# First pair's gates, k, q and v on four quarters of the tokens; x normed in place on VectorE

## The chip, the cores and the metric

The kernel runs on one core of a Trainium2 chip. What counts is its device time in microseconds (us), from one launch to its end; lower is better. The engines named below are TensorE (PE: matmuls and transposes by the identity; PEld is its weight load), VectorE (DVE), ScalarE (ACT), GpSimd (POOL) and SyncE (SP), whose queue issues the DMA transfers.

## The reference

One decoder layer for 1024 tokens of width 1024, in float32. The part that matters here is its beginning: the tokens are RMS-normed, projected by `w_in`, and the FoX heads attend with a forget bias.

```
h = rms_norm(x, g_attn[l])          # x * rsqrt(mean(x*x) + eps) * g
z = h @ w_in[l]
(fq, fk, fv, f_logit, nq, kc, vc, ksl, vsl, kwn, vwn, n_gate, g_a, g_b) = jnp.split(z, offsets, axis=-1)
o_fox = fox_attention(fox_h(fq), fox_h(fk), fox_h(fv), f_logit, b_forget[l])
...
log_f = jax.nn.log_sigmoid(f_logit + b_f)        # in fox_attention
c = jnp.cumsum(log_f, axis=1).transpose(0, 2, 1)
s = jnp.einsum('bhqd,bkhd->bhqk', qi, k) * SCALE + ci[..., None] - c[:, :, None, :]
```

The second branch (NSA), the merge, the squared-ReLU MLP and the final norm follow; the change does not touch them.

## The kernel before

Every float32 product is made from a high and a low part (`float32r`), in three passes: low weights by high data, high by low, high by high. The normed tokens stand transposed in `hT`: `hTh[0]`, `hTl[0]` hold the high and low part of tokens 0 to 511 (half 0), `hTh[1]`, `hTl[1]` those of half 1; each is 128 partitions by 8 blocks of the width by 512 tokens.

`phase_a` makes `hT`. For each of eight tiles `i` of 128 tokens, x is loaded; `xg = x * g` is made, fifteen of the sixteen half rows on GpSimd; ScalarE squares x with a running sum, and `rstd` and `newton` make the factor `r` of each token by five small VectorE instructions (`v`, `y`, `t`, `t`, `r`) of one column. For tiles 0 to 2 (`NDIAG`), a diagonal matrix `by = identity * r` is made and the transposing matmul multiplies by it; for the others VectorE scales `xg` by `r`, and TensorE transposes by the identity `idn`. `turn_tile` then copies four 128x128 blocks at a time from PSUM (tile `tn_...`, two banks) to `hTh` on ScalarE and subtracts on VectorE for `hTl`.

A `Steps` list holds pieces of TensorE work with a cost each. `gates` (the forget and NSA gate logits, tile `g`), `k_pair` (`fk`), `q_pair` (`fq`) and `v_pair` (`fv`) fill the lists `qa`, `qb`, `s1` for the first pair of heads. `proj` does 24 matmuls for one projection of 512 tokens; with `parts=2` it does them as two sets of 24 with 256 tokens each. Before, half 0 of the gates, k and q is done in such quarters: quarter 0 (tiles 0, 1) in `qa`, quarter 1 (tiles 2, 3) in `qb`; half 1 and all of v stand in `s1`, 512 tokens wide. `phase_a` runs `qa` beside tiles 2 and 3, and `qb` beside tiles 4 to 7; `s1` follows. The raw weights come by DMA (`wload`, two buffers `wr`) and are split into `wh_...` on ScalarE and `wl_...` on VectorE (`wsplit`).

A scheduler orders the instructions of each engine from the order of the code and these lists; at run time each engine works through its own row in that order and waits at its head. After the first pair's projections, `attend` interleaves the attention of the heads (scores `sf`, softmax `pf`, transposes `ptf`, `accs`) with the projections of the next pairs (`f1`). The softmax needs `cb`, the cumulated log forget gate, which goes through DRAM: gates, `turn`, `logf`, `back` (transposes `lfT`), `cumsum`, the transfers `c_d` and `cb`. `rel_tables` makes the tables of the relative bias for the later NSA stage; it ends with 16 strided copies `yy<-u`.

Of the kernel before, what the change touches and what calls it, by code (L numbers as in the profile page):

```python
# [10 lines left out]
F32 = mybir.dt.float32  # L11
# [113 lines left out]
class Kernel:  # L125
# [63 lines left out]
    def wsplit(self, n):  # L189
        nc = self.nc  # L190
        while len(self.wdone) <= min(n, len(self.seq) - 1):
            m = len(self.wdone)
            _, name, shape, pool, gates = self.wq[self.seq[m]]
            raw = self.wloaded[m]
            if gates:
                st = self.wp.tile([P, 8, P], FR, tag="wh", bufs=self.SPL, name="wh_g")
                nc.vector.tensor_copy(st[:, :, 64:128], self.zero[:, 0:64].unsqueeze(1).to_broadcast([P, 8, 64]))
                nc.scalar.copy(st[:, :, 0:32], raw)
                nc.vector.tensor_sub(st[:, :, 32:64], raw, st[:, :, 0:32].bitcast(F32))
                self.wdone.append((st, None))  # L200
# [8 lines left out]
    RAW, SPL = 2, 3  # L209
    VT, VTN = 2, 3  # L210
# [22 lines left out]
    def consts(self):  # L233
# [17 lines left out]
        pt = self.psS("rowsT")  # L251
# [41 lines left out]
    def turn_tile(self, y, half, j, name, by=None):  # L293


        nc = self.nc
        hi, lo = self.hT[half]

        def one(c):
            pt = self.psT(f"tn_{name}_{c}")  # L300
            for k in range(4):
                if by is None:
                    self.tr(pt[:, k * P:(k + 1) * P], y[c][:, k * P:(k + 1) * P], self.idn)
                else:
                    self.mm(pt[:, k * P:(k + 1) * P], y[c][:, k * P:(k + 1) * P], by, start=True, stop=True)
# [32 lines left out]
    def proj_half(self, st, n, half, name, done, psf=None):  # L338
        if len(st) == 3 and half == 0:
            self.proj(st, n, half, name, done, psf, parts=2)  # L340
        else:
            self.proj(st[-1], n, half, name, done, psf)


    def phase_a(self, qa, qb):
# [27 lines left out]
        self.idents()  # L373
        self.wload(1)
        load(2)
        load(3)
        cut = lambda l, k, n: l[k * len(l) // n:(k + 1) * len(l) // n]
        with_ = {2: cut(qa, 0, 2), 3: cut(qa, 1, 2), **{k + 4: cut(qb, k, 4) for k in range(4)}}
        for i in range(8):
            if i == 2:  # L380
                self.wload(2)
                for k in range(4, 8):
                    load(k)
            junk = fp.tile([P, T], F32, tag="P1", bufs=2, name=f"junk_{i}")
# [12 lines left out]
            t = self.turn_tile([xg[:, 0:H], xg[:, H:D]], i // 4, i % 4, f"a{i}", by)  # L397
            run(interleave(t, with_.get(i, [])))
            if i == 7:
                self.consts()  # L400

    WARM = 12
    NDIAG = 3
    GDVE = ((0, 1),)

    def gates(self, st):
# [6 lines left out]
        def mats(half, q, nq):  # L413
# [8 lines left out]
            if q == nq - 1:  # L422
                tmp = self.att.tile([32, H], F32, tag="vt", bufs=self.VT, name=f"gt{half}")
                nc.scalar.copy(tmp, ps[32:64])
                gz = self.att.tile([32, H], F32, tag="vt", bufs=self.VT, name=f"gz{half}")
                nc.vector.tensor_add(gz, ps[0:32], tmp)
                gt = self.psS(f"gT{half}")
                box["gz", half] = gz
                box["gt", half] = gt

        def turn(half):
            gz, gt = box["gz", half], box["gt", half]
# [34 lines left out]
        def back(half):  # L467
# [3 lines left out]
            pt = self.psS(f"lfT{half}")  # L471
# [26 lines left out]
        for half in range(2):  # L498
            st[2].after(2000, 4 * 30, lambda half=half: turn(half))
        for half in range(2):  # L500
            st[2].after(st[2].wait() + 2500 * (1 - half), 4 * 60, lambda half=half: back(half))

    def rel_tables(self):
# [8 lines left out]
        pt = self.psS("rel")  # L512
# [4 lines left out]
        pf = self.psS("relf")  # L517
# [622 lines left out]
    def attention(self):  # L1140
# [6 lines left out]
        def fox_qkv(st, p):  # L1147
# [12 lines left out]
        qa, qb, s1, f1 = Steps(), Steps(), Steps(), Steps()  # L1160
        self.gates((qa, qb, s1))
        pairs = [fox_qkv((qa, qb, s1), 0)]
        self.commit(qa)
        self.commit(qb)
        self.commit(s1)
# [779 lines left out]
```

## Time and profile before

| | |
|---|---|
| time, median of 3 runs | 1627.71 us (1626.15 to 1630.89) |
| the profiled execution | 1629.54 us, of which the span of the profile is 1627.5 us |
| PE busy | 1590.8 us (98%), 8245 matmuls |
| DVE, ACT, POOL busy | 1095.3, 855.6, 381.3 us |
| mean granted clock of TensorE | 0.989 of full speed |

The page's slices show TensorE busy in tenths: 7 in the first of 40 slices (0 to 41 us), 9 in all others but the last; the granted clock is 7 tenths in that first slice and 9 or more in all others. A stretch of a few microseconds is read from the trace by windows, in which the busy time of each engine, the granted clock and the DMA traffic stand side by side.

### The profile page before, as it was taken

The page shows a single profiled execution, that of the slowest core. Times are in us where ns is not written, and L with a number is a line of the kernel's source. Part 1 is how long each engine was busy: PE and PEld are TensorE (multiplying, and loading weights), DVE is VectorE, ACT ScalarE, POOL GpSimd, SP SyncE. Part 2 cuts the span into 40 slices and gives each one's busy share as a digit, 9 for nine tenths or more (in the row PEclk, how much of TensorE's full clock was granted, in tenths as well). Part 3 has the DMA queues.
Part 4 walks back from the last instruction along what each step waited for, and adds up shares of the span by engine and source line. Part 5 has one row for each costly group of instructions (what it writes and reads, how often), then busy time and mean ns, then how long its engine had stood idle before and what let it go on. Part 6 is the DMA issues. An engine that isn't in the chain of part 4 may idle for free. (4 is left out here: it accounts for less than half of the span.)

```text
span 1627.5 us, 23814 instructions
## 1 busy us (share of the span) xinstructions
PE 1590.8 (98%) x8245; PEld 1348.5 (83%) x8245; DVE 1095.3 (67%) x2355; ACT 855.6 (53%) x1632; POOL 381.3 (23%) x466
## 2 busy tenths in 40 slices
PE   7999999999999999999999999999999999999997
PEld 5888888888888888898888878788888878888886
DVE  8556666765665565666766569666666689787876
ACT  4456565655555565667653246655555544333334
POOL 7122122212233222336430000333333100000004
PEclk7999999999999999999999999999999999999999
DMA  5321211342122211213437743454444596445312
GB/s 173 60 69 35 61 48 49 111 103 68 57 66 75 65 32 45 85 58 117 147 113 249 256 154 117 143 182 155 149 153 158 187 350 207 155 151 169 108 52 104
DMA packets 165232, 196.68 MB, mean 121 GB/s; under 512 B 21289, under 2 KB 100969, under 8 KB 165105
## 3 DMA queue, kind: packets, MB, share of 16 engines
q1 hardware_dynamic: 165112, 195.18, 37.9%
q8 instruction: 65, 1.06, 0.3%
q14 instruction: 55, 0.44, 0.1%
HBM read 139.99 MB, written 55.15 MB: 120 GB/s over the span
## 5 line engine op out<-in xcount | busy, mean ns | idle before, releaser
L157 PE MATMUL oX<-to,so 128*128 128x512 f32 x672 | 154.8, 389 | 0.0
L157 PEld LDWEIGHTS oX<-to,so 128*128 128x128 f32 x672 | 126.1, 188 | 26.2
L1776 ACT CAST to<-w 128x1024 fp32r<-128x1024 f32 x48 | 48.2, 1051 | 150.6 <-PE accs L157 59.8
L820 DVE TENSOR_TENSOR PTn<-ptn,PTn 128x512 fp32r<-128x512 f32 (+2 forms) x136 | 81.9, 609 | 51.8 <-ACT PTn L819 51.3
L819 ACT CAST PTn<-ptn 128x512 fp32r<-128x512 f32 (+2 forms) x136 | 69.2, 521 | 55.5 <-PE ptn L160 49.4
L1614 POOL TENSOR_TENSOR ss<-w 128x512 f32<-128x512 f32 x15 | 24.2, 1616 | 316.4 <-DMA w<-in_w_ff_dram 200.8
L157 PE MATMUL fX<-ht,w1h 128*128 128x512 f32 x384 | 95.0, 389 | 0.0
L1886 POOL TENSOR_TENSOR z<-x,gf 128x512 f32<-128x512 f32 x14 | 18.7, 1355 | 309.5 <-DVE x L1825 305.3
L157 PE MATMUL accs<-PTn,Vnv 128*128 128x256 f32 x480 | 91.0, 305 | 0.0
L796 POOL TENSOR_SCALAR pf<-pf,rdf 128x896 f32<-128x896 f32 (+3 forms) x64 | 47.4, 748 | 178.7 <-DVE rdf L795 154.1
L157 PEld LDWEIGHTS fX<-ht,w1h 128*128 128x128 f32 x384 | 72.0, 188 | 15.4 <-DVE ht L1493 0.5
L157 PE MATMUL g<-hTl,wh_g 128*128 128x512 f32 (+1 forms) x280 | 78.6, 402 | 0.0
L157 PE MATMUL oZ<-to,so 128*128 128x512 f32 x336 | 77.5, 389 | 0.0
L1605 DVE TENSOR_TENSOR w1l<-w,w1h 128x1024 fp32r<-128x1024 f32 (+1 forms) x32 | 34.6, 1082 | 59.9 <-ACT w1h L1604 59.9
L157 PEld LDWEIGHTS accs<-PTn,Vnv 128*128 128x128 f32 x480 | 72.3, 189 | 2.7 <-DVE otn L829 0.4
L157 PEld LDWEIGHTS oZ<-to,so 128*128 128x128 f32 x336 | 63.1, 188 | 13.1
L157 PE MATMUL g<-hTh,wh_g 128*128 128x512 f32 (+1 forms) x280 | 73.2, 389 | 0.0
L157 PE MATMUL g<-hTh,wl_g 128*128 128x512 f32 x256 | 71.9, 399 | 0.0
L1777 DVE TENSOR_TENSOR so<-hr,so 128x1024 fp32r<-128x1024 f32 x56 | 68.2, 1240 | 2.4 <-ACT so L1776 2.4
L1776 ACT CAST so<-hr 128x1024 fp32r<-128x1024 f32 x56 | 56.6, 1049 | 12.9 <-DMA hr<-hid_d 12.8
L1777 DVE TENSOR_TENSOR to<-w,to 128x1024 fp32r<-128x1024 f32 x48 | 56.7, 1223 | 7.7 <-ACT to L1776 7.7
L793 ACT ACTIVATE pf<-pf,mf 128x896 f32<-128x896 f32 (+3 forms) x64 | 49.5, 774 | 20.4 <-DVE mf L780 17.5
(528 smaller groups left out, 4354.7 us busy)
## 6 DMA issues: line engine op xcount, KB each, us to landing
w<-in_w_ff_dram SPq DMA_DIRECT2D x62, 512.0 KB, 4.6
hr<-hid_d SPq DMA_DIRECT2D x56, 512.0 KB, 4.3
wr_wo<-in_w_out_dram SPq DMA_DIRECT2D x20, 512.0 KB, 3.9
x<-in_x_dram SPq DMA_DIRECT2D x16, 512.0 KB, 6.8
wr_g<-in_w_in_dram SPq DMA_DIRECT2D x16, 512.0 KB, 3.8
hid_d<-h22s SPq DMA_DIRECT2D x32, 256.0 KB, 2.5
hid_d<-s2s SPq DMA_DIRECT2D x32, 256.0 KB, 2.0
hid_d<-s3h SPq DMA_DIRECT2D x32, 256.0 KB, 2.2
```

Of the source, the lines that this page charges most:

```text
L157: self.last = self.nc.tensor.matmul(*a, **k)
L793: nc.scalar.activation(p, p, AF.Exp, bias=nm, scale=-1.0, accum_out=den)
L796: nc.gpsimd.tensor_scalar(p, p, r, 1.0 if gate is None else gate, op0=OP.mult, op1=OP.mult)
L819: nc.scalar.copy(th, src)
L820: nc.vector.tensor_sub(tl, src, th.bitcast(F32))
L1605: nc.vector.tensor_sub(lo, src, hi.bitcast(F32))
L1614: e.tensor_add(p[:, 4:8], b[:, 0:4], b[:, 4:8])
L1776: nc.scalar.copy(o[:, 0, s], src)
L1777: nc.vector.tensor_sub(o[:, 1, s], src, o[:, 0, s].bitcast(F32))
L1886: nc.gpsimd.tensor_mul(y[:, c], x[:, c], gf[:, c])
```

## The change

The first pair's lists become four, one for each quarter of 256 tokens, for gates, k, q and v alike. Tiles 0 and 1 are normed and turned first; then quarter 0 is cut in three and run beside tiles 2, 3 and 4, quarter 1 beside tiles 5, 6 and 7; quarters 2 and 3 follow. `norm` writes x in place with two VectorE instructions per tile (`x * r * g`, 512 columns each); the GpSimd products and the diagonal matrices go. The weights of v are split into buffers of their own (`PT`), and v and q use the PSUM banks `S`. The weight of k is loaded behind the third tile of x, no longer ahead of it. The 16 copies `yy` go from GpSimd to ScalarE, and `wcap` keeps the next pair's weights from being split before quarter 3.

```diff
     def wsplit(self, n):
-        while len(self.wdone) <= min(n, len(self.seq) - 1):
+        while len(self.wdone) <= min(n, len(self.seq) - 1, self.wcap):
...
     def proj_half(self, st, n, half, name, done, psf=None):
-        if len(st) == 3 and half == 0:
-            self.proj(st, n, half, name, done, psf, parts=2)
+        if len(st) == 4:
+            self.proj(st[2 * half:], n, half, name, done, psf, parts=2)
...
-    def phase_a(self, qa, qb):
+    def phase_a(self, qs):
...
+        self.wload(0)
+        load(2)
         self.wload(1)
-        load(2)
         load(3)
-        cut = lambda l, k, n: l[k * len(l) // n:(k + 1) * len(l) // n]
-        with_ = {2: cut(qa, 0, 2), 3: cut(qa, 1, 2), **{k + 4: cut(qb, k, 4) for k in range(4)}}
-        for i in range(8):
-            if i == 2:
-                self.wload(2)
-                for k in range(4, 8):
-                    load(k)
+
+        def tile_(i):
             junk = fp.tile([P, T], F32, tag="P1", bufs=2, name=f"junk_{i}")
-            xg = fp.tile([P, T], F32, tag="PT" if i % 2 else "Q", bufs=3 if i % 2 else 4, name=f"xg_{i}")
-            for c in range(2):
-                cs = slice(c * H, c * H + H)
-                eng = nc.vector if (i, c) in self.GDVE else nc.gpsimd
-                eng.tensor_mul(xg[:, cs], xts[i][:, cs], gb[:, cs])
-            r = self.rstd(xts[i], junk, f"a{i}")
-            by = None
-            if i < self.NDIAG:
-                by = fp.tile([P, P], F32, tag="ot", bufs=3, name=f"by{i}")
-                nc.vector.tensor_scalar(by, self.idn, r, None, op0=OP.mult)
+            y = [xts[i][:, c * H:c * H + H] for c in range(2)]
+            self.norm(xts[i], y, [gb[:, 0:H], gb[:, H:T]], junk, f"a{i}")
+            return self.turn_tile(y, i // 4, i % 4, f"a{i}")
...
+        for i in range(2):
+            run(tile_(i))
+        self.wsplit(1)
+        q0, q1 = split(qs[0], self.AT0), split(qs[1], self.AT1_)
+        for i, w in enumerate(q0 + q1):
+            if i < 6:
+                t = tile_(i + 2)
+                if i == 0:
+                    for k in range(4, 8):
+                        load(k)
+                run(interleave(w, t, 1.0))
             else:
-                nc.vector.tensor_scalar(xg, xg, r, None, op0=OP.mult)
-            t = self.turn_tile([xg[:, 0:H], xg[:, H:D]], i // 4, i % 4, f"a{i}", by)
-            run(interleave(t, with_.get(i, [])))
-            if i == 7:
+                run(w)
+            if i == 5:
                 self.consts()
...
-    NDIAG = 3
-    GDVE = ((0, 1),)
+    AT0 = (0.33, 0.67)
+    AT1_ = (0.33, 0.67)
...
-        for q in range(2):
-            st[q].add(8 * MM, lambda q=q: mats(0, q, 2), n)
-        st[2].add(16 * MM, lambda: mats(1, 0, 1), n)
+        for q in range(3):
+            st[q].add(8 * MM, lambda q=q: mats(q // 2, q % 2, 2), n)
+        st[2].after(0, 4 * 30, lambda: turn(0))
+
+        def rest():
+            st[2].add(8 * MM, lambda: mats(1, 1, 2), n)
+            st[2].after(2000, 4 * 30, lambda: turn(1))
...
         for b in range(16):
-            nc.gpsimd.tensor_scalar(y[:, b, 0:127], u[:, 15 - b:15 - b + 16 * 126 + 1:16], 1.0, 1.0,
-                                    op0=OP.mult, op1=OP.mult)
+            nc.scalar.copy(y[:, b, 0:127], u[:, 15 - b:15 - b + 16 * 126 + 1:16])
```

How the instructions stand on the engines: first VectorE, from the first tiles on. Before, this stands behind the matrix `by` of tile 0 (`hTl_83` is the low part of half 0, `r_a` the factor of a tile).

```order
L309 TENSOR_TENSOR hTl_83<-tn_a_0_145,hTh_82 128x4x128
L394 TENSOR_SCALAR by_176<-idn,r_a_174 128x128
L206 TENSOR_TENSOR wl_fk_231<-wr_fk_121,wh_fk_230 128x1024
L309 TENSOR_TENSOR hTl_83<-tn_a_1_152,hTh_82 128x4x128
L267 TENSOR_SCALAR v_a_208<-ss_a_204 128x1
L309 TENSOR_TENSOR hTl_83<-tn_a_0_178,hTh_82 128x4x128
```

In the changed kernel this row of VectorE stands between the square sum of tile 2 (`ss_a_195`) and the first low part of tile 1 (`tn_a_0_172`); `x_106` is the buffer of tiles 0 and 1, `x_121` that of tiles 2 and 3.

```order
L269 TENSOR_SCALAR v_a_199<-ss_a_195 128x1
L293 SCALAR_TENSOR_TENSOR x_106<-x_106,r_a_168,g_attn_b 128x512 x2
L276 RECIPROCAL y_a_201<-sq_a_197 128x1
L207 TENSOR_TENSOR wl_fk_191<-wr_fk_123,wh_fk_190 128x1024
L279 SCALAR_TENSOR_TENSOR t_a_203<-y_a_201,v_a_199 128x1
L269 TENSOR_SCALAR v_a_279<-ss_a_275 128x1
L280 TENSOR_SCALAR t_a_203<-t_a_203 128x1
L282 TENSOR_TENSOR r_a_206<-y_a_201,t_a_203 128x1
L293 SCALAR_TENSOR_TENSOR x_121<-x_121,r_a_206,g_attn_b 128x512
L307 TENSOR_TENSOR hTl_83<-tn_a_0_172,hTh_82 128x4x128
```

The norm of tile 1 now stands behind the square sum of tile 2, and the split of k's weight and half of tile 2's norm stand ahead of tile 1's low part.

TensorE before, from the first gate matmuls (`g`) on, with the transposes of tile 2 (`tn_a_0_219`, `tn_a_1_264`), tile 3 (`xg_288`) and the tables between quarter 0 and quarter 1:

```order
L157 MATMUL g_236<-hTl_83,wh_g 128x256 x4
L157 MATMUL fk_0_259<-hTh_82,wl_fk_231 128x256 x8
L157 MATMUL fk_0_259<-hTl_83,wh_fk_230 128x256 x4
L157 MATMUL tn_a_0_219<-by_217,xg_201 128x128 x4
L157 MATMUL g_236<-hTl_83,wh_g 128x256 x4
L157 MATMUL g_236<-hTh_82,wh_g 128x256 x8
L157 MATMUL tn_a_1_264<-by_217,xg_201 128x128 x4
L157 MATMUL fk_0_259<-hTl_83,wh_fk_230 128x256 x4
L157 MATMUL fk_0_259<-hTh_82,wh_fk_230 128x256 x8
L160 MATMUL tn_a_0_305<-idn,xg_288 128x128 x4
L160 MATMUL tn_a_1_335<-idn,xg_288 128x128 x4
```

TensorE in the changed kernel, the same place from the second half of tile 2's transposes to tile 4's first (`x_210`):

```order
L160 MATMUL tn_a_1_255<-idn,x_121 128x128 x4
L157 MATMUL fk_0_250<-hTl_83,wh_fk_190 128x256 x4
L157 MATMUL fk_0_250<-hTh_82,wh_fk_190 128x256 x4
L160 MATMUL tn_a_0_294<-idn,x_121 128x128 x4
L157 MATMUL fk_0_250<-hTh_82,wh_fk_190 128x256 x4
L157 MATMUL accs<-reltmp 8x130
L157 MATMUL fq_0_311<-hTh_82,wl_fq_245 128x256 x8
L157 MATMUL fq_0_311<-hTl_83,wh_fq_244 128x256 x8
L157 MATMUL fq_0_311<-hTh_82,wh_fq_244 128x256 x8
L160 MATMUL tn_a_1_320<-idn,x_121 128x128 x4
```

Quarter 0 now carries 24 matmuls of q here (and 24 of v behind them) between the transposes, where before tile 3's two groups of transposes followed each other.

ScalarE in the changed kernel, around the copies `yy` (`hTh_84` is half 1, so the row behind them belongs to tile 4):

```order
L306 CAST hTh_82<-tn_a_1_255 128x4x128
L206 CAST wh_fv_305<-wr_fv_218 128x1024
L306 CAST hTh_82<-tn_a_0_294 128x4x128
L306 CAST hTh_82<-tn_a_1_320 128x4x128
L547 COPY yy<-u 8x127 x16
L306 CAST hTh_84<-tn_a_0_359 128x4x128
L306 CAST hTh_84<-tn_a_1_381 128x4x128
```

The sixteen copies stood on GpSimd before; now they stand ahead of tile 4's high part. From the second head of the first pair on, the rows of all engines read as before, but for their buffer numbers.

## Rows read from the trace of the kernel before

**Rows 1.** Windows: busy us of each engine (instructions), granted clock, DMA share, GB/s.
```profile
6.20:11.20 5.00, 0.00 (x0) 0.02 (x1) 4.38 (x7) 1.64 (x4) 4.21 (x3) 0.78 0.89 201
11.20:20.40 9.20, 7.43 (x32) 6.91 (x32) 7.31 (x14) 4.98 (x9) 7.19 (x6) 0.50 1.04 388
20.40:28.50 8.10, 7.82 (x58) 7.61 (x57) 7.82 (x15) 5.93 (x14) 8.10 (x8) 0.86 0.32 75
28.50:33.30 4.80, 1.80 (x11) 1.07 (x11) 4.73 (x20) 2.95 (x7) 3.12 (x5) 0.95 0.01 2
33.30:40.00 6.70, 6.70 (x31) 6.37 (x31) 6.09 (x16) 0.66 (x2) 2.62 (x6) 0.52 0.29 79
40.00:51.00 11.00, 10.97 (x94) 10.56 (x93) 5.37 (x8) 6.60 (x11) 5.46 (x16) 1.00 0.47 50
51.00:57.00 6.00, 3.87 (x12) 3.22 (x13) 2.87 (x5) 2.92 (x6) 0.00 (x0) 0.72 0.51 53
57.00:85.58 28.58, 27.63 (x133) 21.99 (x131) 15.43 (x24) 11.30 (x18) 1.26 (x2) 1.00 0.24 64
85.58:200.00 114.42, 114.25 (x661) 97.14 (x660) 71.60 (x183) 69.51 (x141) 25.58 (x36) 1.00 0.19 52
```

**Rows 2.** Timeline: start us, us, engine, line, operation; the pair's end on TensorE.
```profile
85.16 0.42 PEld L160 LDWEIGHTS vTfv<-idn,vtfv 128*128 128x128 f32 x4 [1.10 <-ACT vtfv L601]
...
85.58 2.09 PE L157 MATMUL fk<-hTh,wl_fk 128*128 128x512 f32 x8
```

**Rows 3.** Window of the score tile sf: PE, PEld, DVE, clock, DMA.
```profile
70.00:85.58 15.58, 1.92 (x7) 1.06 (x6) 0.00 (x0) 1.00 0.28 77
```

**Rows 4.** Timeline: weight loads of consecutive matmuls at full clock.
```profile
42.72 1.01 PEld L157 LDWEIGHTS fq<-hTh,wl_fq 128*128 128x128 f32 x8
...
45.60 0.46 PEld L160 LDWEIGHTS tn_a<-idn,xg 128*128 128x128 f32 x4
...
65.11 1.68 PEld L157 LDWEIGHTS fq<-hTh,wl_fq 128*128 128x128 f32 x8
...
70.46 1.77 PEld L157 LDWEIGHTS fv<-hTh,wl_fv 128*128 128x128 f32 x8
```

**Rows 5.** Groups by form: busy us, mean ns of one, idle before.
```profile
L389 POOL TENSOR_TENSOR xg<-x,g_attn_b 128x512 f32<-128x512 f32 x15 | 20.5, 1401 | 4.7 <-DMA g_attn_b<-in_g_attn_dram 2.5 <-DMA x<-in_x_dram 2.2
L309 DVE TENSOR_TENSOR hTl<-tn_a,hTh 128x512 fp32r<-128x512 f32 x16 | 10.9, 685 | 4.1 <-ACT hTh L308 4.1
L277 DVE SCALAR_TENSOR_TENSOR t_a<-y_a,v_a 128x1 f32<-128x1 f32 x8 | 4.6, 578 | 0.2
L280 DVE TENSOR_TENSOR r_a<-y_a,t_a 128x1 f32<-128x1 f32 x8 | 4.2, 522 | 0.2
L274 DVE RECIPROCAL y_a<-sq_a 128x1 f32<-128x1 f32 x8 | 1.2, 152 | 0.2 <-ACT sq_a L265 0.2
L206 DVE TENSOR_TENSOR wl_fq<-wr_fq,wh_fq 128x1024 fp32r<-128x1024 f32 x1 | 1.2, 1204 | 0.0
L277 DVE SCALAR_TENSOR_TENSOR t_m<-y_m,v_m 128x1 f32<-128x1 f32 x8 | 1.7, 217 | 0.1
```

**Rows 6.** Timeline of the MLP's norm on VectorE.
```profile
948.39 1.42 DVE L1445 SCALAR_TENSOR_TENSOR x<-x,r_m,g_mlp_b 128x512 f32<-128x512 f32 x2
```

**Rows 7.** Timeline: first instructions that waited for tiles 1 and 2 of x.
```profile
8.01 1.06 ACT L263 ACTIVATE junk<-x 128x1024 f32<-128x1024 f32 x1 [2.21 <-DMA x<-in_x_dram]
8.98 0.19 ACT L263 ACTIVATION_READ_ACCUMULATOR junk<-x 128x1 f32 x1
...
13.21 8.40 POOL L389 TENSOR_TENSOR xg<-x,g_attn_b 128x512 f32<-128x512 f32 x6 [2.23 <-DMA x<-in_x_dram]
```

**Rows 8.** The tile yy: duration ns min/median/max, first and last start us.
```profile
L537 POOL TENSOR_SCALAR yy<-u x16: 390/398/1166, 37.4 to 43.8; 8x127 f32<-8x127 f32 x16
```

**Rows 9.** Timeline of the forget bias: last lfT copy, its transfer, the first softmax.
```profile
77.37 0.68 DVE L474 COPY lfT<-lfT 8x512 f32<-8x512 f32 x1 [0.17 <-PE lfT L160]
...
81.98 0.29 SPq L493 DMA_DIRECT2D c_d<-cs  x1
...
87.47 0.62 DVE L780 CUSTOM_DVE_ANT_0 pf<-sf,cb 128x448 f32<-128x448 f32 x1 [2.73 <-DMA cb<-c_d]
```

More of the change, by code (lines that the diff above doesn't have):

```diff
@@ L301, in one @@
             for k in range(4):
[L302 to L305, printed above, removed]
+                self.tr(pt[:, k * P:(k + 1) * P], y[c][:, k * P:(k + 1) * P], self.idn)
             pv = pt.rearrange("p (k t) -> p k t", k=4)
@@ new lines, in tile_, with split @@
+        def tile_(i):
+            junk = fp.tile([P, T], F32, tag="P1", bufs=2, name=f"junk_{i}")
+            y = [xts[i][:, c * H:c * H + H] for c in range(2)]
+            self.norm(xts[i], y, [gb[:, 0:H], gb[:, H:T]], junk, f"a{i}")
+            return self.turn_tile(y, i // 4, i % 4, f"a{i}")
+        def split(steps, at):
+            tot, c, k, out = sum(c for c, _ in steps), 0.0, 0, [[]]
+            for e in steps:
+                if k < len(at) and c >= at[k] * tot:
+                    k += 1
+                    out.append([])
+                out[-1].append(e)
+                c += e[0]
+            return out
@@ L422, in mats @@
             if q == nq - 1:
[L423 to L429, printed above, removed]
+                if half == 0:
+                    box["gz"] = [self.att.tile([32, 2, H], F32, tag="Q", bufs=4, name=f"gz{i}") for i in range(2)]
+                gz = box["gz"][half]
+                nc.scalar.copy(gz[:, 1], ps[32:64])
+                nc.vector.tensor_add(gz[:, 0], ps[0:32], gz[:, 1])
         def turn(half):
-            gz, gt = box["gz", half], box["gt", half]
+            gz, gt = box["gz"][half][:, 0], self.psT(f"gT{half}")
             gv = gt[:, 0:P].rearrange("p (i c) -> p i c", c=32)
@@ L470, in back @@
             xf = box["xf"]
-            pt = self.psS(f"lfT{half}")
+            pt = self.psT(f"lfT{half}")
             for j in range(4):
@@ L493, in cumsum @@
             nc.sync.dma_start(self.c_d, c)
-        for q in range(2):
-            st[q].add(8 * MM, lambda q=q: mats(0, q, 2), n)
-        st[2].add(16 * MM, lambda: mats(1, 0, 1), n)
[L498 to L501, printed above, removed]
+        for q in range(3):
[4 more added lines that the diff above has]
+            st[2].after(2000, 4 * 30, lambda: turn(1))
+            for half in range(2):
+                st[2].after(st[2].wait() + 3500 * (1 - half), 4 * 60, lambda half=half: back(half))
+        return rest
     def rel_tables(self):
@@ L589, in k_pair, with v_pair @@
                 late.append(len(st[-1].steps))
-    def v_pair(self, st, parts, name, out, bufs):
+    def v_pair(self, st, parts, name, out, bufs, psf=None, pool=None):
         nc = self.nc
-        n = self.wadd(parts, name)
+        n = self.wadd(parts, name, pool=pool)
         box = {}
@@ L605, in turn @@
             vt = box[half]
-            pt = self.psP(f"vT{name}{half}")
+            pt = (self.psP if psf is None else self.psT)(f"vT{name}{half}")
             for j in range(4):
@@ L614, in v_pair @@
         for half in range(2):
-            self.proj_half(st, n, half, name, lambda ps, half=half: done(half, ps))
-            st[-1].after(1500, 4 * TR, lambda half=half: turn(half))
+            self.proj_half(st, n, half, name, lambda ps, half=half: done(half, ps), psf)
+            if len(st) < 4:
+                st[-1].after(1500, 4 * TR, lambda half=half: turn(half))
+            else:
+                st[2 + half].after(2000, 4 * TR, lambda half=half: turn(half))
     def compress(self, st, c0, w1, w2, pecol, name, last):
@@ L1153, in alloc @@
                 return out["k"]
+            psf = self.psS if len(st) == 4 else None
             self.k_pair(st, [(None, self.wcols(O_FK + p * P))], f"fk{p}", alloc)
-            self.q_pair(st, O_FQ + p * P, f"fq{p}", out, 4)
-            self.v_pair(st[-1:], [(None, self.wcols(O_FV + p * P))], f"fv{p}", out, 2)
-            return out
[L1160 to L1165, printed above, removed]
+            if rest is not None:
+                rest()
+            self.q_pair(st, O_FQ + p * P, f"fq{p}", out, 4, psf)
+            self.v_pair(st, [(None, self.wcols(O_FV + p * P))], f"fv{p}", out, 2, psf,
+                        (lambda: (self.att, "PT", 3)) if psf else None)
+            return out
+        qs4, f1 = [Steps() for _ in range(4)], Steps()
+        pairs = [fox_qkv(qs4, 0, self.gates(qs4))]
+        for st in qs4:
+            self.commit(st)
         gl = [(O_GA, f, self.ga_d) for f in range(8)] + [(O_GB, f, self.gb_d) for f in range(8)]
```

27 lines of the change are left out of this document (15 added, 12 removed).

## The prediction

> **What bounds the kernel now.** I read the page first: TensorE is busy 98% of the span, and only the first slice shows it slack. Then I cut the beginning into windows [rows 1]. The reader is to look at three columns: TensorE's busy time, its clock, and who else is busy. From 85.58 us on TensorE is busy 114.25 of 114.42 us at full clock, so whatever it gains before then is gained at the end, and other engines matter only where they make it wait. Before that point there are three holes. Until 11.2 us it has no data. From 11.2 to 20.4 it does the first three tiles' transposes with gaps, at clock 0.50, the lower of its two levels (1.2 GHz); GpSimd is busy 7.19 us of these 9.2. From 28.5 to 33.3 it is busy 1.80 of 4.80 us, while VectorE is busy 4.73; the clock is then at 0.52 until 40. From 51 to 57 it is busy 3.87 of 6 us at clock 0.72. The cause in all of them is that quarter 0 offers TensorE too little work while the tiles come slowly: each tile needs two GpSimd products of 1.40 us, and VectorE's tiny instructions take 0.578 and 0.522 us on average here, against 0.217 for the same step in the MLP's norm, where GpSimd multiplies nothing [rows 5].
>
> **The mark.** I compare both kernels where the first pair is done and TensorE starts the k projection of the second pair: 85.58 us [rows 2]. Before, the scores of three blocks stand ahead of it (1.06 us of weight loads [rows 3]) and a second group of v's transposes (0.46 us, as any such group [rows 4]), which stand behind it in the changed order. So the time to beat is 85.58 - 1.06 - 0.46 = 84.1 us.
>
> **The change, part by part.**
>
> *TensorE's work.* Twenty-four matmuls of 256 columns take 45.60 - 42.72 = 2.88 us, 0.120 each; twenty-four of 512 take 70.46 - 65.11 = 5.35 us, 0.223 each [rows 4]. The four quarters hold 4 x 88 = 352 matmuls of 256: 352 x 0.120 = 42.2 us. Going from 512 to 256 columns adds 2 x 0.120 - 0.223 = 0.017 us a pair, for 112 pairs (half 1 and both halves of v) 1.9 us. The Trainium skill ("VectorE: DVE Perf Modes", the section on the TRN2 errata) gives a matmul max(60, 6 + columns) cycles of 2.4 GHz, 0.109 us for 256; an estimate by that page would make the 352 cheaper by 3.8 us. The trace differs, with 0.120 us where a weight load stands before each, and the row decides. Twelve groups of transposes for tiles 2 to 7 at 0.46 make 5.5 us; some 25 small ones (gates, log gates, v, tables) at the transposes' 0.115 make 2.9. Together 50.6 us at full clock.
>
> *When it can start.* The diagonal matrices and GpSimd's products go; in their place VectorE does two instructions a tile at 1.42 / 2 = 0.71 us [rows 6]. Quarter 0 starts when tile 1's first low part is there. On VectorE that stands behind the square sum of tile 2, thus behind tile 2's landing. Before, tile 2 landed at 13.21 us [rows 7] with k's weight (512 KB) ahead of it; at 388 GB/s [rows 1] 0.52 MB take 1.4 us, so without it 11.8; the other bound is tile 1's 8.0 plus 1.4 = 9.4. I take 11.8, since the DMA engines are 0.89 to 1.04 busy there [rows 1]. The square and its read-out take 1.2 us [rows 7], and then VectorE has: a small instruction, two norm halves, the reciprocal, k's split of 1.2 us, four small ones, half of tile 2's norm, and the low part of 0.69 [rows 5], in all 1.42 + 1.2 + 0.71 + 0.69 + 6 x 0.17 = 5.1 us (0.17 lies between 0.152 and 0.217 [rows 5]). Start: 11.8 + 1.2 + 5.1 = 18.1 us; bounds 15.7 and 19.5.
>
> *The clock.* At 18 us TensorE has again been mostly idle, so it starts at the lower level. Stretches at that level lasted, by the windows' means, some 13 us in the first stage (most of it without continuous work), 6.8 around 33 to 40, and 3.4 around 53 to 57 [rows 1]. Half of 3.4 to 6.8 us is lost; I take 2.5.
>
> *Does VectorE keep up?* From the norm of tile 1 (13.0 us) to tile 7's last low part it has 14 norm halves (9.9 us), 14 low parts (9.7), three weight splits (3.6), 31 small ones (5.3), five of 0.69 for gates, k and q (3.5), the tables (1.9): 33.9 us, so 47 us if it never waits. TensorE reaches tile 7's transposes after 195 matmuls and eleven groups: 18.1 + 2.5 + 23.4 + 5.1 + 0.5 = 49.6 us. So VectorE is ahead by some 2 us, no more, and short waits are likely (q's weight split stands behind four tiles' work). I add 1.0 for these and the copies below, with 0 and 4 as bounds.
>
> *The copies yy.* GpSimd's took 0.398 us each in the median and 1.17 at most [rows 8]. On ScalarE they stand ahead of tile 4's high part. They wait for VectorE's table u, which has 13.0 + ten norm halves (7.1), five low parts (3.4), three splits (3.6), 27 small ones (4.6) and 1.1 of tables ahead: 32.8 us. At 0.398 they end at 39.2, and tile 4's first high and low part (0.6 and 0.69) at 40.5. TensorE needs the bank that this frees for tile 5, after 131 matmuls and six groups: 18.1 + 2.5 + 15.7 + 2.8 + 0.3 = 39.4 us. So copies of 0.33 us or less are hidden by TensorE's work on the first two quarters, 0.398 cost the 1.1 that I have added, and beyond that they cost their full time.
>
> *Moved at no cost.* The weights' transfers: q's and v's are issued behind x, at 14 to 16 us, and needed from 24 us on; the DMA share is 0.32 or less from 20.4 us [rows 1]. PSUM banks and the in-place x: their readers are done tiles earlier.
>
> *Sum.* 18.1 + 50.6 + 2.5 + 1.0 = 72.2 us against 84.1: 11.9 us gained. The profiled execution, 1629.5 us (span 1627.5 and 2.0 around it), becomes 1617.6. It lies 1.8 us above the median of the runs; 1627.7 - 11.9 gives **1616 us**.
>
> **Rivals.**
>
> *The copies stall ScalarE.* If each took GpSimd's slowest 1.17 us [rows 8], they would end at 51.5, tile 5's transposes would stand 13.4 us on TensorE, and the clock would fall once more (2 us): 72.2 - 1.0 + 13.4 + 2 = 86.6 at the mark, 2.5 us later than before, which is no change by the bound below. For it: every element read lies 16 floats from the last. Against: the median on GpSimd is 0.398. The Trainium skill ("SBUF — State Buffer", the section on door 1) says that each access to a new 16-byte line pays a penalty, and these reads change line at each element; no row here shows it on ScalarE.
>
> *VectorE paces.* If its tiny instructions stay at 0.5 us instead of 0.17, as beside GpSimd's products [rows 5], the 31 cost 10 us more, less the 2 to 3 us of lead: mark at about 79, time 1622 to 1623. Against: GpSimd reads nothing in this stage but k's copies.
>
> *More is gained.* Tile 2 lands at 9.4 and the clock rises early: 15.7 + 50.6 + 1.5 = 68, time 1611.
>
> *Slower: the forget bias is late.* From the last lfT copy to the first softmax took 87.47 - 77.37 = 10.1 us [rows 9]. In the new order two weight splits (1.2 each), k's and q's last parts (three of 0.69) and one of v's stand between on VectorE: some 15 to 16 us. TensorE's cover behind lfT is 31 matmuls of 256 (3.7 us), both halves of the second pair's k (48 x 0.223 = 10.7), scores and transposes (2.0): 16.4 us. Each microsecond beyond costs one; to end slower by over 4.9 us, the chain would have to take 33 us. Even at double its length it would only cancel the gain.
>
> **How the numbers follow.** 0.3% of the time is 4.9 us, about what this measurement can tell from no change. Chances: the forecast with a mark of 69 to 75.5 us, 1612.5 to 1619.5, 0.70; VectorE pacing, 1619.5 to 1623, 0.13 (0.12 of it faster); more gained 0.08; copies stalling or VectorE worse than this, no change, 0.06; slower by the forget bias 0.03. So faster 0.90, same 0.07, slower 0.03. The range 1610 to 1622 leaves out the no-change and slower cases, half of the gainers and part of VectorE's.
>
> **What would show it.** TensorE continuous from 18 us (start wrong: no gate matmuls before 20); clock full from about 23 to the end; VectorE's tiny instructions near 0.17 us; yy on ScalarE near 0.3 to 0.4 us, tile 4's high part not later than 40; no TensorE wait over 1 us between 18 us and the mark; the mark near 72 with nothing given back behind it. The prediction is wrong if TensorE waits at tile 5's transposes or at q's first weights, or if the first softmax makes it wait.

## The result

The changed kernel takes 1620.74 us in the median of 6 runs (1618.98 to 1623.31) against 1629.78 (1626.15 to 1631.47) of the kernel before, run beside it: ratio 0.9948, 95% interval 0.9934 to 0.9962, 9.0 us gained. The forecast was 1616 us, range 1610 to 1622.

The first fence has windows of the changed kernel, with the columns of [rows 1]. The second has rows of TensorE's timeline: the first product, the first product of the second pair's k (the mark of the prediction; before [rows 2]), the transposes of the first two softmaxes, and the first product of the third pair's k, which I use below as a second mark. The third has that last row in the kernel before.

```profile
17.00:20.00 3.00, 3.00 (x14) 3.00 (x15) 2.96 (x13) 3.00 (x9) 0.00 (x0) 0.50 0.81 268
20.00:69.54 49.54, 49.54 (x414) 48.33 (x413) 31.45 (x71) 29.96 (x58) 3.96 (x9) 1.00 0.38 75
69.54:88.65 19.11, 18.86 (x92) 14.79 (x90) 12.15 (x24) 9.42 (x15) 2.86 (x4) 1.00 0.20 58
88.65:95.10 6.45, 4.00 (x14) 3.32 (x15) 3.32 (x7) 3.59 (x10) 2.54 (x4) 0.74 0.30 81
```

```profile
16.99 0.79 PE L157 MATMUL g<-hTl,wh_g 128*128 128x256 f32 x2 [1.99 <-DVE hTl L307]
...
69.54 2.10 PE L157 MATMUL fk<-hTh,wl_fk 128*128 128x512 f32 x8
...
87.14 0.44 PE L160 MATMUL ptf<-idn,pf 128*128 128x128 f32 x2
...
91.10 1.04 PE L160 MATMUL ptf<-idn,pf 128*128 128x128 f32 x6 [2.46 <-POOL pf L808]
...
127.50 2.10 PE L157 MATMUL fk<-hTh,wl_fk 128*128 128x512 f32 x8
```

```profile
136.51 2.07 PE L157 MATMUL fk<-hTh,wl_fk 128*128 128x512 f32 x8
```

The front became what it was meant to be: from 17.0 us to the mark TensorE has no hole (3.00 of 3.00 and 49.54 of 49.54 us), and the mark stands at 69.54, 14.6 us ahead of the comparable 84.1. But at the second mark only 136.51 - 127.50 = 9.0 us of this are left, and the span is 8.1 us shorter (1627.5 to 1619.4). Between the marks 5.5 us were given back. The window from 88.65 to 95.10 shows where: TensorE waits 2.46 us for the second softmax, and then runs some 3.4 us at the lower clock (0.74 over the window).

That softmax stands at the end of a chain that begins with the forget bias. The next fence follows it over the engines: VectorE's copies of lfT and the two scans with what stands between them, the store `c_d` and the load `cb` on SP's queue, the first softmax's first subtraction and its reciprocal, the second softmax's last subtraction, exponentials and reciprocals with the weight split between them, and GpSimd's division, which released the transposes at 91.10 (before: [rows 9]).

```profile
66.34 1.27 DVE L480 COPY lfT<-lfT 8x512 f32<-8x512 f32 x2
...
69.08 2.28 DVE L490 TENSOR_TENSOR_SCAN cs<-on,lfT 8x1024 f32<-8x1024 f32 x1
...
71.29 1.19 DVE L207 TENSOR_TENSOR wl_fv<-wr_fv,wh_fv 128x1024 fp32r<-128x1024 f32 x1
72.51 0.69 DVE L566 SCALAR_TENSOR_TENSOR Qfq<-fq,Qfq 64x512 fp32r<-64x512 f32 x1
73.23 0.21 DVE L495 TENSOR_TENSOR_SCAN sc<-sc,cs 8x32 f32<-8x32 f32 x1
73.48 0.69 DVE L621 TENSOR_TENSOR Vfv<-vTfv,Vfv 128x512 fp32r<-128x512 f32 x1
74.08 1.17 DVE L496 TENSOR_TENSOR cs<-cs,sc 8x992 f32<-8x992 f32 x1
...
75.28 0.29 SPq L499 DMA_DIRECT2D c_d<-cs  x1
77.14 0.34 SPq L904 DMA_DIRECT2D cb<-c_d  x1
...
80.83 0.62 DVE L792 CUSTOM_DVE_ANT_0 pf<-sf,cb 128x448 f32<-128x448 f32 x1 [4.00 <-DMA cb<-c_d]
...
85.75 0.16 DVE L807 RECIPROCAL rdf<-denf 128x1 f32<-128x1 f32 x1 [1.75 <-ACT pf L805]
85.94 0.75 DVE L792 CUSTOM_DVE_ANT_0 pf<-sf,cb,mf 128x512 f32<-128x512 f32 x1
...
86.94 1.05 ACT L206 CAST wh_fk<-wr_fk 128x1024 fp32r<-128x1024 f32 x1
...
87.89 1.15 ACT L805 ACTIVATE pf<-pf,mf 128x1024 f32<-128x1024 f32 x1
...
88.01 1.68 DVE L207 TENSOR_TENSOR wl_fk<-wr_fk,wh_fk 128x1024 fp32r<-128x1024 f32 x1 [0.16 <-ACT wh_fk L206]
...
89.03 0.39 ACT L805 ACTIVATE pf<-pf,mf 128x128 f32<-128x128 f32 x1
...
89.62 0.21 DVE L807 RECIPROCAL rdf<-denf 128x1 f32<-128x1 f32 x2
...
89.93 1.93 POOL L808 TENSOR_SCALAR pf<-pf,rdf 128x1024 f32<-128x1024 f32 x3 [1.31 <-DVE rdf L807]
```

Three steps of the chain itself take 2.28, 0.21 and 1.17 us, but the store follows the copies' end (67.61) only 7.7 us later: k's, q's and v's last parts and a weight split of the second pair stand between. Behind the bias, too, other work stands in the row: the second softmax's last subtraction is behind the first one's reciprocal, for which VectorE stood idle 1.75 us, and the split of the third pair's k weight is ahead of the exponential on ScalarE (1.05 us) and of the reciprocal on VectorE (1.68 us).

### The profile page after: what moved, and what is told of

It reads as the page before. It is cut to its first block, busy times and chain, and to the rows that moved or that the text cites. A ratio compares the mean times of both kernels' runs of the same rounds, so it can differ in the third digit from the quotient of the medians.

```text
span 1619.4 us, 23977 instructions
## 1 busy us (share of the span) xinstructions
PE 1586.4 (98%) x8333; PEld 1348.5 (83%) x8333; DVE 1089.0 (67%) x2362; ACT 860.7 (53%) x1648; POOL 355.6 (22%) x435
## 5 line engine op out<-in xcount | busy, mean ns | idle before, releaser
L1629 POOL TENSOR_TENSOR ss<-w 128x512 f32<-128x512 f32 x15 | 24.2, 1610 | 317.0 <-DMA w<-in_w_ff_dram 197.3
L805 ACT ACTIVATE pn<-pn,mn 128x896 f32<-128x896 f32 (+3 forms) x64 | 49.6, 776 | 19.4 <-DVE mn L792 19.0
```

What stands on the lines that cost most here:

```text
L805: nc.scalar.activation(p, p, AF.Exp, bias=nm, scale=-1.0, accum_out=den)
L1629: e.tensor_add(p[:, 4:8], b[:, 0:4], b[:, 4:8])
```

## The experiments

The theory after the two traces: everything up to the mark was gained, and the late forget bias takes 5 us back. Rivals: the copies and splits that bunch up on ScalarE and VectorE take it back whatever the bias does, or the clock does. The table holds, for the profiled execution of each kernel, the mark, the first softmax's first subtraction (when the bias is there) and the second mark, the last two as distances from the first mark, since the mark itself differs by up to 1.3 us between executions with the same front (69.54 to 70.82); TensorE's busy time and mean clock from 69.5 to 105 us; and the times. In the kernel before and in e1, 1.5 us of scores and transposes stand ahead of the mark that stand behind it in the others: on the others' footing their second marks are at +52.45, and part of their 35.5 us, as of e2's, lies ahead of the mark. The diffs leave out lines that only set up names, and shorten some (`...`).

| kernel | mark | bias | 2nd mark | busy of 35.5, clock | median us | ratio to before, 95% |
|---|---|---|---|---|---|---|
| before | 85.58 | +1.89 | +50.93 | 34.82, 1.00 | 1629.78 | |
| changed | 69.54 | +11.29 | +57.96 | 32.79, 0.95 | 1620.74 | 0.9948 (0.9934-0.9962) |
| e1 norm alone | 76.35 | +1.94 | +50.93 | 34.82, 1.00 | 1621.37 | 0.9958 (0.9945-0.9971) |
| e2 quarters alone | 73.09 | +10.59 | +55.82 | 32.95, 1.00 | 1620.85 | 0.9955 (0.9941-0.9968) |
| e3 yy on GpSimd | 70.91 | +11.33 | +56.39 | 32.74, 1.00 | 1621.01 | 0.9961 (0.9947-0.9976) |
| e4 no bias wait | 69.78 | +5.94 | +52.90 | 35.50, 1.00 | 1616.03 | 0.9928 (0.9913-0.9943) |
| e5 one more hop | 70.82 | +13.54 | +59.17 | 31.84, 0.95 | 1620.81 | 0.9967 (0.9954-0.9980) |
| e6 splits on GpSimd | 70.34 | +11.18 | +57.33 | 32.30, 1.00 | 1621.07 | 0.9955 (0.9942-0.9968) |
| e8 splits later | 70.11 | +9.08 | +54.97 | 34.04, 1.00 | 1619.58 | 0.9952 (0.9940-0.9964) |
| e9 gates first | 70.88 | +10.14 | +56.46 | 33.78, 0.95 | 1619.85 | 0.9956 (0.9944-0.9967) |
| e10 loads behind | 70.44 | +8.27 | +54.50 | 34.57, 1.00 | 1619.90 | 0.9957 (0.9942-0.9971) |
| e11 halves | 69.85 | +9.13 | +55.57 | 33.80, 1.00 | 1619.21 | 0.9953 (0.9938-0.9967) |
| e12 changed again | 70.41 | +11.19 | +57.94 | 32.77, 0.95 | 1620.03 | 0.9951 (0.9937-0.9965) |
| e13 loads behind again | 69.78 | +9.66 | +55.89 | 33.47, 1.00 | 1618.99 | 0.9948 (0.9934-0.9962) |

The kernel before took 1629.78 us beside the changed kernel, 1629.70 us beside e1, e2, e4 and e6, 1627.34 beside e3, e5, e8 and e9, 1628.04 beside e10 and e11, and 1628.42 beside e12 and e13.

**e1, the norm alone.** The kernel before, with

```diff
-            xg = fp.tile(...); eng.tensor_mul(xg[:, cs], xts[i][:, cs], gb[:, cs]); by = ...
+            y = [xts[i][:, c * H:c * H + H] for c in range(2)]
+            self.norm(xts[i], y, [gb[:, 0:H], gb[:, H:T]], junk, f"a{i}")
```

> The kernel before with one part of the change: x normed in place on VectorE, no GpSimd multiply and no diagonal matrices; the token lists stay as they were (gates, k and q of half 0 in quarters, the rest 512 wide). If the two parts are worth what their covers suggest (TensorE waits for tiles as soon as it has no products to put between them), the tiles come faster but TensorE has only some 13 us of products to put among tiles 2 to 7, so it still waits for the last tiles: a gain of 3 to 6 us against before, 1624 to 1627 us. Rival: the norm alone is the whole gain (the quarters only reorder work): 1620 to 1622 us.

Measured 1621.37 us: the rival's number, but not its reason. TensorE does wait for tiles, as the theory says (53.14 of 56.35 us busy before the mark, where the changed kernel is full), and the mark is 6.8 us later than with the quarters, 5.3 on the same footing. Behind it there is no wait at all:

```profile
20.00:76.35 56.35, 53.14 (x322) 45.84 (x321) 37.34 (x79) 27.14 (x47) 11.11 (x25) 0.97 0.36 72
76.35:105.00 28.65, 28.65 (x154) 23.95 (x153) 16.92 (x43) 17.08 (x32) 6.20 (x9) 1.00 0.18 52
```

In this order the scans follow each other (68.91, 71.29, 71.54), the store begins at 72.74, 2.5 us earlier than in the changed kernel, and the subtraction comes at 78.29. The second mark is at +50.93, as in the kernel before, so nothing is given back, and e1 (127.28) stands there level with the changed kernel (127.50).

**e2, the quarters alone.** The changed kernel, with `xg` on GpSimd and the diagonal matrices as before.

> The changed kernel with the norm as before (GpSimd multiplies x by g, the first three tiles turned through a diagonal matrix), and k, q, v and the gates on four quarters. If GpSimd's pace is hidden behind the added products, only the later start counts: quarter 0 begins 2 to 4 us later than in the changed kernel, a good part of it at the low clock, and later waits are small: 1622 to 1625 us. Rival: GpSimd's pace reaches TensorE anyway (some 2.8 us of multiplies a tile, plus what waits behind them): over 1626 us, hardly a gain on before.

Measured 1620.85 us, less than the 1622 to 1625 expected. Quarter 0 begins 1.5 us later than in the changed kernel (18.52), at full clock, and TensorE waits 1.8 us from 20 to 69 us. The mark comes 3.6 us later, and 1.4 us are left of this at the second mark. The gains of the parts (8.3 and 8.9 us) do not add up to more than either: behind the mark all three kernels come to the same place, 127.3 to 128.9 us.

**e3, the copies yy.** 

```diff
-            nc.scalar.copy(y[:, b, 0:127], u[:, ...:16])
+            nc.gpsimd.tensor_scalar(y[:, b, 0:127], u[:, ...:16], 1.0, 1.0, op0=OP.mult, op1=OP.mult)
```

> The changed kernel with the 16 copies of yy back on GpSimd, the third thing that the change moves. ScalarE then has 5.2 us less to do among tiles 2 to 5, where TensorE did not wait in the changed kernel; GpSimd takes 16 times 1.17 us and nothing reads yy before the second stage. Theory: the copies are covered, no change, 1620 to 1621.5 us. Rival: ScalarE's copies stand in front of tile copies, and taking them away gains 1 us or more; or GpSimd's long run of copies slows VectorE beside it and loses 1 us or more.

Measured 1621.01 us, no difference: TensorE is busy 49.00 of 49.00 us from 20 to 69, so the copies are covered on either engine.

**e4, no wait for the bias.** The forget bias that is added is rows of x.

```diff
-                nc.sync.dma_start(self.cb, ap(self.c_d, h * T, [[0, P], [1, T]]))
+                nc.sync.dma_start(self.cb, ap(a_x, h * T, [[0, P], [1, T]]))
```

> The changed kernel, but the forget bias that the softmax of the fox units adds is loaded from rows of x and not from the summed forget gates (the gates are still computed and stored; the bias values are others). The first softmax then waits for no chain of VectorE steps and no DMA behind them. Theory: what was given back behind the mark is the late forget bias: the wait of 2.46 us before the second softmax's transposes and the low clock behind it go, and the time falls by 3.5 to 5.5 us against the changed kernel, to 1615 to 1617 us. Rival: it is given back by the copies and splits that bunch up on ScalarE and VectorE, or by the clock after 70 us at full speed, whatever the bias does: within 1 us of the changed kernel, 1619.5 to 1621.5 us.

Measured 1616.03 us, ratio 0.9928, 4.8 to 5.3 us below e1, e2 and e6 on the same chip. The splits, the copies and the whole chain on VectorE up to the store are still there; the wait is gone:

```profile
69.78 2.10 PE L157 MATMUL fk<-hTh,wl_fk 128*128 128x512 f32 x8
...
82.54 0.38 PE L160 MATMUL ptf<-idn,pf 128*128 128x128 f32 x2
82.57 1.15 ACT L805 ACTIVATE pf<-pf,mf 128x1024 f32<-128x1024 f32 x1
...
86.76 1.06 ACT L206 CAST wh_fk<-wr_fk 128x1024 fp32r<-128x1024 f32 x1
...
87.04 0.82 PE L160 MATMUL ptf<-idn,pf 128*128 128x128 f32 x6
...
122.68 2.07 PE L157 MATMUL fk<-hTh,wl_fk 128*128 128x512 f32 x8
```

The second softmax's transposes come 17.3 us behind the mark instead of 21.6, TensorE is busy 35.50 of 35.50 us, the clock stays full, and the second mark is 136.51 - 122.68 = 13.8 us ahead of before, 13.7 in the medians. So the late bias is the main cause; copies and splits that bunch up whatever the bias does are not.

Two things changed along with the wait. The clock stayed full; e3 has the changed kernel's wait at full clock and its second mark at +56.39, so about 1.6 us of the 5.1 between the changed kernel and e4 go with the clock and 3.5 with the wait. And the split of the third pair's k weight stands behind the second softmax's exponential in e4 (86.76 and 82.57), ahead of it in the changed kernel (86.94 and 87.89). In e6 below it stands behind as well, with the bias as late as in the changed kernel, and TensorE is no busier. So a late bias makes TensorE wait without this split; what the split adds to the wait in the changed kernel was not measured.

**e5, the bias later.**

```diff
-            nc.sync.dma_start(self.c_d, c)
+            nc.sync.dma_start(c1, c)
+            nc.sync.dma_start(self.c_d, c1)
```

> The changed kernel with one more copy of the forget bias from DRAM to DRAM ahead of its loads, so that it is there some 2 to 3 us later and nothing else differs. Theory (the bias is what TensorE waits for behind the mark): each us that it is later is a us at the end, 1622.5 to 1624.5 us, and the waits ahead of the second softmax's transposes grow by 2 to 3 us in all. Rival (the wait is of copies and splits on ScalarE and VectorE): within 0.7 us of the changed kernel.

In the profile, which is of the slowest run, the bias comes 2.25 us later and the second mark 1.2 us, half of the theory's rate at this end. The median, 1620.81 us over nine runs from 1619.70 to 1627.30, does not tell it from no change, against 1622.5 to 1624.5 expected; the interval of the ratio, 0.9954 to 0.9980, leans to slower. By itself inconclusive.

**e6, the splits on GpSimd.**

```diff
-            nc.vector.tensor_sub(lo, raw, hi.bitcast(F32))
+            (nc.gpsimd if name in ("fq1", "fv1") else nc.vector).tensor_sub(lo, raw, hi.bitcast(F32))
```

> The changed kernel with one edit: the low parts of the second pair's q and v weights are formed on GpSimd, which is idle there, and not on VectorE, where they stood in the middle of the forget-bias chain (1.38 us ahead of its copies and 1.2 us between its two scans). Theory: the bias is 2.5 to 3.5 us earlier, the wait before the second softmax's transposes falls below 0.5 us: 1616 to 1618 us. Rival: nothing moves, since the chain is not what TensorE waits for, or the slower splits on GpSimd are the next wait: 1620 to 1622 us.

Measured 1621.07 us; the theory's number missed, since the bias did not come earlier (+11.18). The store was issued 4.59 us behind the mark, only 1.15 us earlier than in the changed kernel, because VectorE's scans and GpSimd waited for each other; and the load, with a weight load issued between it and the store, took this back: 4.8 us from issue to use, 3.7 in the changed kernel. TensorE waits for the first softmax's transposes here:

```profile
68.06 2.66 DVE L490 TENSOR_TENSOR_SCAN cs<-on,lfT 8x1024 f32<-8x1024 f32 x1
...
71.46 2.23 DVE L495 TENSOR_TENSOR_SCAN sc<-sc,cs 8x32 f32<-8x32 f32 x1
...
68.66 2.47 POOL L589 TENSOR_SCALAR Kf<-Kf 64x512 fp32r<-64x512 f32 x1
71.22 2.40 POOL L207 TENSOR_TENSOR wl_fv<-wr_fv,wh_fv 128x1024 fp32r<-128x1024 f32 x1
...
74.93 0.29 SPq L499 DMA_DIRECT2D c_d<-cs  x1
75.33 0.37 SPq L186 DMA_DIRECT2D wr_fq<-in_w_in_dram  x1
76.72 0.34 SPq L904 DMA_DIRECT2D cb<-c_d  x1
...
86.86 0.44 PE L160 MATMUL ptf<-idn,pf 128*128 128x128 f32 x2 [1.42 <-POOL pf L808]
...
91.83 1.05 ACT L206 CAST wh_fk<-wr_fk 128x1024 fp32r<-128x1024 f32 x1
```

The second scan, 0.21 us in the changed kernel, lasts until GpSimd's split is done (71.22 + 2.40 = 73.62), and GpSimd's copy of k, 0.61 us elsewhere, begins in the first scan and lasts until 0.4 us behind its end.

**e8, the splits later.** Splits of the second pair's q and v stand behind the last VectorE step of the bias.

```diff
+            with self.tc.issue_after(self.cs.ins) if name in ("fq1", "fv1") else nullcontext():
                 nc.scalar.copy(hi, raw)
                 nc.vector.tensor_sub(lo, raw, hi.bitcast(F32))
```

> The changed kernel with one edit: the splits of the second pair's q and v weights (ScalarE's and VectorE's part) are placed behind the last VectorE step of the forget bias. VectorE's chain from the transposes to the store of the bias then holds 1.38 + 1.2 us less, and GpSimd is not beside the scans. Theory: the store begins 2.5 to 4 us earlier than in the changed kernel (75.3 us there), the first softmax's subtraction follows it, and 2 to 3.5 us come back at the end: 1617 to 1619 us. Rival: the load's way through the DMA queue takes up the difference, as it did with the splits on GpSimd: 1620 to 1621.5 us.

Half of it came, in the profile. Counted from the mark, the store begins 3.5 us earlier, but the bias only 2.2 us (+9.08): weight loads of 512 KB now stand in the queue on both sides of its load:

```profile
72.31 0.29 SPq L500 DMA_DIRECT2D c_d<-cs  x1
73.49 0.37 SPq L186 DMA_DIRECT2D wr_fk<-in_w_in_dram  x1
74.14 0.35 SPq L905 DMA_DIRECT2D cb<-c_d  x1
74.58 0.38 SPq L186 DMA_DIRECT2D wr_fq<-in_w_in_dram  x1
...
79.19 0.62 DVE L793 CUSTOM_DVE_ANT_0 pf<-sf,cb 128x448 f32<-128x448 f32 x1 [3.31 <-DMA cb<-c_d]
```

From issue to use the load takes 5.0 us, 3.7 in the changed kernel. The wait for the transposes falls from 2.46 to 0.7 us, the second mark comes 3.0 us earlier. The median is 1619.58, 7.8 us below the kernel before on the same chip, so no gain over the changed kernel's 9.0 shows in the time.

**e9, the gates first.** As e8, and `rest()` stands ahead of `self.k_pair(...)`.

> As the kernel with the later splits, and the last quarter's gates are written ahead of half 1's k and not behind it, so that the scheduler may turn the forget gates earlier (by three 256-wide products in its order, some 0.4 us). Theory: as the later splits or up to 0.7 us less, 1616.5 to 1618.5 us. Rival: no difference from the later splits within 0.5 us.

Measured 1619.85 us, not 1616.5 to 1618.5. The earlier gates bring the store 0.4 us forward (1.83 us behind the mark, 2.20 in e8), as meant, but the load is issued 2.9 us behind the store (72.71, 75.65), 1.8 in e8, and takes 5.4 us to its use (81.02). What the gates are worth without this is not shown.

**e10 and e11, the loads behind the bias.** As e8, and

```diff
+                with self.tc.issue_after(self.cb0.ins) if name in ("fk2", "fq2") else nullcontext():
                     self.nc.sync.dma_start(raw if sl is None else raw[:, :, sl], src)
```

where `cb0` is the load of the first head's bias; in e11 that load has two pieces, of 448 and 576 columns.

> As the kernel with the later splits, and the two weight loads that the splits set free (half a megabyte each) stand behind the load of the first head's bias in the DMA queue and not beside it. In the later splits the bias was stored 3 us earlier than in the changed kernel, but its load took 5.0 us from issue to use there against 3.7. Theory: the load takes 3.7 us again, the first softmax's subtraction comes at about 8.3 us behind the first product of the second pair's k (9.2 in the later splits, 11.3 in the changed kernel), another 0.8 to 1.3 us comes back just behind the first softmaxes, and no wait above 0.3 us is left for them: 1617 to 1619 us. Rival: the first softmaxes now wait for ScalarE and VectorE's other copies, no difference from the later splits.

> As the kernel with the loads behind, and the first head's bias is loaded in two pieces (448 and 576 columns), so that the first subtraction, which needs the first 448, can begin before the rest is there. Theory: if the steps follow the pieces, the first subtraction comes 1 to 1.7 us earlier and up to 1 us comes back: 1616 to 1618.5 us; with no wait left to take away, within 0.5 us of the kernel with the loads behind.

```profile
72.64 0.29 SPq L501 DMA_DIRECT2D c_d<-cs  x1
74.47 0.34 SPq L906 DMA_DIRECT2D cb<-c_d  x1
74.99 0.38 SPq L187 DMA_DIRECT2D wr_fk<-in_w_in_dram  x1
...
78.71 0.62 DVE L794 CUSTOM_DVE_ANT_0 pf<-sf,cb 128x448 f32<-128x448 f32 x1 [2.51 <-DMA cb<-c_d]
```

In e10 the bias comes at +8.27, as expected, with 4.2 us from the load's issue to use (3.7 expected), and the transposes wait 0.3 us. The second mark is at +54.50, 3.5 us better than the changed kernel, 1.6 short of e4. The median, 1619.90, is 8.1 us below the kernel before and shows nothing of it. In e11 the bias comes later than in e10, at +9.13, since the store's issue and the load's stand 3.0 us apart (72.05, 75.09) and 1.8 in e10; whether the two pieces bring anything cannot be told from one execution of each, as e13 shows.

**e12 and e13, both again on one chip.** No edit.

> The changed kernel again, as it is, on the same chip and in the same rounds as the kernel with the loads behind, since their medians so far come from different chips. Expected: 1620 to 1621.5 us, 7 to 9 us below before; in its profile the first products behind the first two softmaxes (105 us) 2.5 us later than with the loads behind, as before.

> The kernel with the later splits and the loads behind, again, beside the changed kernel. If what is won behind the first softmaxes (2.5 us in the profiles) lasts to the end, as the lead of the kernel without the bias wait did: 1.5 to 3 us below the changed kernel. Rival: later waits of the attention stages take it up, within 1 us of the changed kernel.

The changed kernel's distance comes back, +57.94. That of the loads behind does not quite, +55.89 against +54.50: the store's issue and the load's are 3.2 us apart here (71.98, 75.17) and 1.8 in e10, the same kernel, so the bias comes at +9.66 and the transposes wait 1.0 us. Differences of this size among e8 to e11 are thus within what one kernel shows by itself, and that the loads behind improve on e8 is not shown. The medians are 1620.03 and 1618.99 us, 1.0 us apart where the second marks are 2.7 (2.1 of it behind the first mark), with ranges that overlap (1618.52 to 1621.49, 1618.37 to 1622.02). So the better order is not shown to beat the changed kernel in time, only in the profile at 125 us.

## Why the prediction was right or wrong

**The work, right.** From 16.99 to 69.54 us are 52.55 us without a hole, of which 3.00 at the lower clock lost 1.5: 51.05 us at full clock, forecast 50.6. So 0.120 us for a matmul of 256 columns held.

**The start, 1.1 us too late.** Tile 2's square began at 10.94 us (forecast 11.8), and the first product 4.9 us behind its read-out (5.1).

**The clock, 2.5 forecast, 1.5 lost.** It was low from before 17.00 to 20.00 and full after that to the mark.

**Waits and copies, 1.0 forecast, 0 measured.** VectorE's small instructions are short without GpSimd's products beside them, as the step assumed, against 578 and 522 ns [rows 5]. The copies took 5.23 us for sixteen, 0.327 each, just below the 0.33 that the text gave as hidden, and tile 4's high part began at 34.51 us. The groups by form and ScalarE's timeline:

```profile
L279 DVE SCALAR_TENSOR_TENSOR t_a<-y_a,v_a 128x1 f32<-128x1 f32 x8 | 1.7, 213 | 0.1
L282 DVE TENSOR_TENSOR r_a<-y_a,t_a 128x1 f32<-128x1 f32 x8 | 1.2, 147 | 0.1
```

```profile
29.37 5.23 ACT L547 COPY yy<-u 8x127 f32<-8x127 f32 x16 [0.21 <-DVE u L536]
34.51 1.05 ACT L306 CAST hTh<-tn_a 128x512 fp32r<-128x512 f32 x2
```

The rival that the copies stall ScalarE thus fails on its price. It drew on the penalty for each new line that the Trainium skill ("SBUF — State Buffer", door 1) states without a size. One such copy of 127 elements lasts 0.413 us in the median; the nearest row with adjacent elements, another operation, is the exponential over 128 at 89.03, 0.39 us. So no penalty of weight is seen here, though no copy of adjacent elements measures it. Together these steps put the mark at 69.5 (70.4 in e12), not 72.2.

**"Nothing given back behind the mark", wrong.** This is the step that failed: 5.5 us came back. With it fails the opening rule of the forecast, that what is gained before 85.58 is gained at the end, and the forecast's own sign of being wrong was met, by the second softmax and not the first. Its mechanism stood among the rivals, "the forget bias is late". That rival had the chain right (15 to 16 us forecast from the copies of lfT to the first softmax; 66.97, the last copy's start as half of the row at 66.34, to 80.83 is 13.9), and the cover wrong at its end: it asked whether TensorE has work until the first subtraction, and TensorE had. What TensorE waits for are the second softmax's transposes, 10.3 us behind that subtraction (80.83 to 91.10), with its maximum, exponential, sum and division on three engines, and k's copies and the third pair's weight split between. The price was 2.7 us of idle time (32.79 of 35.50 busy; e4 35.50) and some 1.8 us of clock (0.95 of 35.5), 4.5 of the 5.1 us by which e4's second mark is nearer.

**The sum.** A mark 2.7 us better than forecast and 5.5 us given back make a gain of 9.0 instead of 11.9 us; that the time lies in the range is partly the one error against the other. Within the range it is luck too: 1620.74 lies outside the forecast's own 1612.5 to 1619.5, in the 1619.5 to 1623 that the chances gave to VectorE pacing, which did not happen. (The kernel before ran 2.1 us slower beside the changed one than the 1627.71 that the forecast started from; from there 11.9 us less would have been 1617.9.) With the bias wait taken out the gain is 13.7 us, so the mark was counted rightly. How much of each microsecond of bias comes back is not settled: between e4 and e5 the second mark moves by 0.8 us for each (59.17 - 52.90 over 13.54 - 5.94), against the changed kernel by 0.5 (e5) to 1.4 (e8), and the clock is mixed into this. The second marks of e8 to e11 and e13 are 1.5 to 3.5 us nearer than the changed kernel's, but against the kernel before on their own chips they gain 7.5 to 9.4 us, about as much as the changed kernel's 8.4 (e12) and 9.0. Where their lead goes, later than 127 us, stays open.

## What to carry to other kernels

When a stage ahead of a latency chain is filled up, the chain does not get shorter, and its end, not the stage's, may decide: here either half of the change alone gave nearly the whole gain (8.3 and 8.9 of 9.0 us). Follow such a chain to the instruction at which the bounding engine really waits, not to its first visible stop, and count the cover up to there. Work that has time (the next pair's splits and loads) takes the place of work that has none when it stands in the same engine's or queue's order.

## What the runs showed of the hardware

In e6 a VectorE scan and a GpSimd instruction, both with operands in SBUF, waited for each other's end: 2.23 us instead of 0.21 for the scan, and 2.47 instead of 0.61 for GpSimd's copy. The Trainium skill ("SBUF — State Buffer", "SBUF: two separate sides") says that the pair of ports that the two engines share is held by whoever starts first for the whole instruction; this trace agrees.

The load of the bias, 512 KB, took 3.6 to 3.8 us from issue to use where the nearest weight load was issued over 4 us away (before, changed, e1, e2, e3, e12), 4.2 to 4.3 with two right behind it (e10, e13), 4.8 with one 1.4 us ahead (e6), and 5.0 to 5.4 with one ahead and one right behind (e8, e9).

The clock behind a wait of 2.5 us fell in the changed kernel both times (0.95 over 35.5 us) and stayed full in e3 with the same wait; it stayed full behind 2.31 us in e2 and fell behind 2.12 us in e5. Around 660 to 680 us it fell in one execution of the changed kernel (first row) and not in the other (second row, e12); 9% of these 20 us are up to 1.8 us, so single profiles differ by this much at the end.

```profile
660.00:680.00 20.00, 18.38 (x104) 16.42 (x103) 14.21 (x61) 12.89 (x34) 6.08 (x9) 0.91 0.14 44
```

```profile
660.00:680.00 20.00, 18.26 (x112) 15.92 (x112) 14.49 (x63) 13.77 (x36) 6.25 (x10) 1.00 0.13 44
```
